# Hybrid RWKV-7 / pooling decoder block: the out-projection is split along its contraction and set beside the last quad of heads, and the quads' working tiles get fixed homes

## The chip, the cores and the metric

One core of a Trainium2 chip runs the whole block. The metric is device microseconds of one execution. Before the change three executions took 2462.72, 2460.82 and 2457.50 us, median 2460.82 us.

The engines of the core are named as in the profile: PE (TensorE, with PEld for its weight loads), DVE (VectorE), ACT (ScalarE), POOL (GpSimd) and SP (SyncE, which here issues all DMAs). Each runs its own list of instructions in order; semaphores hold an instruction until what it needs is there.

## The reference

`x` is 512 tokens by 2048, in float32. What is computed:

```
mod = silu(c) @ w_ada + b_ada                  # 6 x 2048: shift, scale, gate, twice
h   = rmsnorm(x) * (1 + sc1) + sh1
p   = h @ w_in                                 # r,k,v (3 x 1024), low-rank inputs (288), pooling input (1024)
y   = rwkv7(p[rwkv part])                      # 16 heads of 64: S = S*w + (S a) b' + v k';  y_t = S r_t
z   = pool(p[pool part])                       # 4 groups, causal means over 2,4,8,16 tokens, 256x256 matmul each
x   = x + gt1 * (concat(y, z) @ w_out)         # contraction over 2048 = 16 tiles of 128
h   = rmsnorm(x) * (1 + sc2) + sh2
x   = x + gt2 * (silu(gate) * val) @ w_down    # [val, gate] = causal conv of width 3 over h @ w_up
out = rmsnorm(x)
```

The recurrence is done in chunks of 64 tokens: in a chunk it is a triangular system, and the chunk states follow one another.

## The kernel before

All activations lie transposed: a tile is 128 features by 512 tokens. A large product is made from three matmuls of rounded parts (`mm3`, L114: high x high, high x low, low x high), so a weight tile of 128x512 (256 KB, loaded to `wraw`, L107) is first cast by ACT to its high part `whi` (L109) and subtracted by DVE to its low part `wlo` (L111). I call these L115, L116 and L117 matmuls of 512 columns **dense**: 48 of them make one output tile of 128x512 over a contraction of 16 tiles.

The program has these stages. First, adaLN shift and scale and the first eight tiles of the in-projection (L201 to L220). Then the stage that the change is about, in one PSUM layout (`mm`: 2 banks for dense outputs, `bt`: 2 double banks for the mixer, `ch`: 1 double bank for its chain):

- 27 more in-projection tiles (`win_tile`, L309). Tiles of r, k, v go through the token shift to DRAM (`win_pair`, L612) and come back a quad later.
- Four **quads** (`quad`, L362), each four heads. A quad has a front (low-rank matmuls L376 and L377, sigmoids, the scan L388, exponentials, norm of k with L405, up to `bt` L417), then scores (L427), transposed copies (L439), then the 16x16 inverses: a block of `sb` goes by DMA to DRAM and back in another layout (`dn`, `nl`, L451 and L453), DVE solves in 28 small steps (L484, L486), 24 DMAs put the inverses and their transposes in DRAM (`dx`, L492 to L494) and two DMAs read them as `X` and `Y` (L497). Two doubling levels on PE follow (L504, L513, L519), then the chain over eight chunks (L538 to L564), the outputs (L571 to L582), the group norm (L588) and the gate (L602 to L605).
- The rest of the adaLN vector, `ada_rest` (L332): 192 loads `war` of 256 KB, each multiplied by `c` and summed by one DVE instruction (L341).
- Four pooling groups (`pool_front`, `pool_back`), each fed from two in-projection tiles that come last.
- The out-projection: 16 mixer tiles `M` (L661), 16 output tiles. Eight outputs are kept in eight PSUM banks and take the contraction in blocks of four tiles (`out_block`, L666), two more follow whole, the last six in half-width matmuls (`out_half`, L759).

After it come the second norm and the MLP, which the change leaves alone.

The order of the instructions on each engine is fixed when the program is built: a list scheduler takes ready instructions, quads and pools at high priority (`hp`, L621), dense work where nothing of those is ready. What can be ready also hangs on tile buffers, which go round in program order. All quad-sized working tiles (4 KB a partition) come from one pool of 12 buffers, `q4` (L232).

Of the kernel before, what the change touches and what calls it, by code (L numbers as in the profile page):

```python
# [46 lines left out]

WIN_ORDER = ["T0", "T1", "T2", "r0", "k0", "v0", "r1", "k1", "v1"]
# [5 lines left out]
MIX_ORDER = [14, 15, 10, 11, 12, 13, 0, 1, 2, 3, 4, 5, 6, 7, 8, 9]  # L54
# [3 lines left out]
def block_kernel(ctx, tc, a, out, stop=None, dbg=None):  # L58
# [46 lines left out]
    def split_weights(src, eng=V):  # L105
        raw = wp.tile([P, WC], F32, tag="wraw", name="wraw", bufs=4)
        nc.sync.dma_start(raw, src)  # L107
        hi = wp.tile([P, WC], F32R, tag="whi", name="whi", bufs=3)
        S.copy(hi, raw)  # L109
        lo = wp.tile([P, WC], F32R, tag="wlo", name="wlo", bufs=3)  # L110
        eng.tensor_tensor(lo, raw, hi[:, :].bitcast(F32), op=ALU.subtract)  # L111
        return hi, lo
# [6 lines left out]
    def project(ps, src, acts, start=True, stop=True, engs=(V,)):  # L119

        n = len(acts)
        for k0 in range(0, n, WC // P):
            wh, wl = split_weights(src[:, k0 * P : k0 * P + WC], engs[k0 // 4 % len(engs)])
            for kk in range(WC // P):
# [47 lines left out]
    if True:  # L172
# [53 lines left out]
        if True:  # L226
# [5 lines left out]
            def quad_tile(name):  # L232
                return ra.tile([P, 2 * (16 + T)], F32, tag="q4", name=name, bufs=12)
# [7 lines left out]
            xg = two(quad_tile("xg"))  # L241
# [13 lines left out]
            rkv0 = [quad_tile(n) for n in "rkv"]  # L255
# [4 lines left out]
    def load_pw(gi):  # L260
        t = ra.tile([P, T], F32, tag="war", name="pw", bufs=3)
        pw = t.rearrange("p (i d) -> p i d", i=2)
# [3 lines left out]
    def padded(name):  # L266
        return quad_tile(name).rearrange("p (x t) -> p x t", x=2)

    def pool_front(gi, upad):
        win = WINS[gi]  # L270
        cur, lo, step = upad, 1, 1
        while step < win:
            nxt = padded("sw")
# [4 lines left out]
        z = two(quad_tile("z"))  # L278
        V.scalar_tensor_tensor(z, cur[:, :, 16:], 1.0 / win, upad[:, :, 16:], op0=ALU.mult, op1=ALU.subtract)
        V.tensor_mul(z[:, :, 0:win], cur[:, :, 16 : 16 + win], prec[:, None, 0:win].to_broadcast([P, 2, win]))  # L280
        V.tensor_sub(z[:, :, 0:win], z[:, :, 0:win], upad[:, :, 16 : 16 + win])
        return z

    def pool_back(gi, z, pw):
        ps = batch()
        mx = two(quad_tile("mxp"))
        for d in range(2):
            for i in range(2):
                PE.matmul(ps[:, d, :], pw[:, i, d * P : (d + 1) * P], z[:, i, :], start=i == 0, stop=i == 1)  # L289
            j = gi * 2 + d  # L290
            S.activation(mx[:, d, :], ps[:, d, :], AF.Identity, bias=drv[:, 35 + j : 36 + j], scale=col("psc", j))
            if gi:
                nc.sync.dma_start(mixd[8 + j], mx[:, d, :])
            else:
                last_mix.append(split_act(14 + d, mx[:, d, :]))
# [19 lines left out]
    HEADS = [(x, h) for h in range(2) for x in range(2)]  # L315

# [8 lines left out]
    dx = tc.dram_tile([2, 2, C, 2 * NK, C], F32, name="dx")  # L325
    for w in range(2):
        nc.sync.dma_start(dx[w].rearrange("s i j t -> (s i) (j t)"), sall[:, :, :, :].rearrange("p x c t -> p (x c t)"))

    cq = [None]
    modq = ra.tile([P, 4, 48], F32, tag="modq", name="modq")  # L330

    def ada_rest(n0, n1):  # L332
        for n in range(n0, n1):
            kq, j = divmod(n, 48)
            if j == 0:
                cq[0] = ra.tile([P, T], F32, tag="cq", name="cq")
                nc.sync.dma_start(cq[0], cact[0:1, kq * T : (kq + 1) * T].partition_broadcast(P))
            wa = ra.tile([P, T], F32, tag="war", name="war", bufs=3)
            nc.sync.dma_start(wa, a["ada2"][kq, j, :, :])
            jk = ra.tile([P, T], BF16, tag="jkr", name="jkr")  # L340
            V.scalar_tensor_tensor(jk, wa, 1.0, cq[0], op0=ALU.mult, op1=ALU.mult,  # L341
# [20 lines left out]
    def quad(g, rkv):  # L362
# [15 lines left out]
        sg = quad_tile("sg")  # L378
        V.memset(lead(sg)[:, :, 0:1], 0.0)
# [3 lines left out]
        al = quad_tile("al")  # L383
        for x in range(2):
            S.activation(two(al)[:, x, :], psal[:, x, :], AF.Sigmoid, bias=c2("a0", x))
        cs = quad_tile("cs")
        n = 2 * NK * (C + 1)
        V.tensor_tensor_scan(cs[:, 0:n], scanm[:, :, :].rearrange("p c t -> p (c t)"), sg[:, 0:n], 0.0,  # L388
                             op0=ALU.mult, op1=ALU.add)
        mid = ra.tile([P, 2 * NK, 1], F32, tag="mid", name="mid")  # L390
        V.tensor_copy(mid, lead(cs)[:, :, C // 2 : C // 2 + 1])
        V.tensor_sub(lead(cs), lead(cs), mid[:, :, :].to_broadcast([P, 2 * NK, C + 1]))
        ep = quad_tile("ep")
        S.activation(ep[:, 0:n], cs[:, 0:n], AF.Exp, scale=-Q)
# [591 lines left out]
```

## Time and profile before

| | us |
|---|---|
| median of three executions | 2460.82 |
| the profiled execution | 2459.58 |
| its span, first to last instruction | 2457.8 |
| PE busy in the span | 2254.7 (92%) |
| DVE busy | 1345.9 (55%) |
| ACT busy | 831.7 (34%) |
| POOL busy | 23.5 (1%) |
| share of the DMA engines (queue q1) | 44.7% |

A row of the timeline gives start, length, engine, line, operation, output <- input, shape and count; what stands in brackets is how long the engine was idle before it and what ended that. In a group or timeline row a matmul's length holds its way through the array, so dense matmuls of 0.39 us start 0.23 us apart. A matmul of 32-bit operands is two instructions in the trace, so `x64` there is 32 in the program. In a table of stretches each engine's busy time is followed by its instruction count; then come the granted PE clock, the share of the 16 DMA engines and the bytes moved.

### The profile page before, as it was taken

What the parts mean: (1) busy time and instruction counts of PE and PEld (TensorE: products, weight loads), DVE (VectorE), ACT (ScalarE), POOL (GpSimd) and SP (SyncE); (2) the same over time, 40 slices, a digit from 0 to 9 for tenths busy, and PEclk for the clock granted to TensorE, in tenths of its full rate; (3) what the DMA queues carried; (4) which work ended last, traced back from release to release, by engine and by line L of the source; (5) the groups of instructions that cost most, each with busy time, mean ns of one, the idle gap of its engine ahead of it and who ended that gap; (6) DMA issues with size and microseconds to landing.
All of it is one profiled execution on the core that took longest, in us unless ns stands there. A gap on an engine that the chain in (4) does not pass through costs nothing.

```text
span 2457.8 us, 36667 instructions
## 1 busy us (share of the span) xinstructions
PE 2254.7 (92%) x14178; PEld 1829.3 (74%) x14178; DVE 1345.9 (55%) x2398; ACT 831.7 (34%) x1351; POOL 23.5 (1%) x26
## 2 busy tenths in 40 slices
PE   4878888888379999999999999999999999999997
PEld 3656566565257889987888888888888888888887
DVE  7987686766434457757634443444344434444457
ACT  3243252523233335532223322333233322323333
POOL 0000000000000001100000000000000000000000
PEclk9989899999679999999999999999999999999998
DMA  9965757656103635538532233333323332332335
GB/s 357 340 221 163 240 176 222 213 177 208 40 32 120 198 111 181 190 105 260 170 98 98 95 98 96 99 96 97 97 97 99 95 99 95 98 97 97 99 97 174
DMA packets 204418, 352.98 MB, mean 144 GB/s; under 512 B 46033, under 2 KB 52049, under 8 KB 200017
## 3 DMA queue, kind: packets, MB, share of 16 engines
q1 hardware_dynamic: 204242, 350.63, 44.7%
q8 instruction: 111, 1.82, 0.3%
q14 instruction: 65, 0.53, 0.1%
HBM read 335.33 MB, written 15.21 MB: 143 GB/s over the span
## 4 chain that ended last, share of the span: by engine, by line
PE 63%; DMA 2%; DVE 2%; ACT 0%; issue 0%; POOL 0%; DVEq 0%; SPq 0%; ACTq 0%; POOLq 0%
PE b L115 20%; PE b L117 19%; PE b L116 19%; DMA slot<-ada 1%; DMA wraw<-wup 1%; PE bt L115 1%; PE bt L117 1%; PE bt L116 1%; DVE slot L810 1%; PE mm L115 0%; PE mm L117 0%; PE mm L116 0%; DVE wlo L111 0%; PE bt L289 0%; DVE x L863 0%
## 5 line engine op out<-in xcount | busy, mean ns | idle before, releaser
L111 DVE TENSOR_TENSOR wlo<-wraw,whi 128x512 fp32r<-128x512 f32 x772 | 532.3, 692 | 714.9 <-ACT whi L109 700.4
L109 ACT CAST whi<-wraw 128x512 fp32r<-128x512 f32 x788 | 488.5, 622 | 1240.7 <-PE b L116 931.2
L117 PE MATMUL b<-hh,wlo 128*128 128x512 f32 (+1 forms) x1472 | 560.6, 381 | 7.1 <-DVE wlo L111 6.8
L115 PE MATMUL b<-hh,whi 128*128 128x512 f32 (+1 forms) x1472 | 559.9, 380 | 0.0
L116 PE MATMUL b<-hl,whi 128*128 128x512 f32 (+1 forms) x1472 | 559.5, 380 | 0.0
L115 PE MATMUL b<-ah,whi 128*128 128x512 f32 (+1 forms) x992 | 353.3, 357 | 1.9 <-ACT whi L109 1.9
L117 PE MATMUL b<-ah,wlo 128*128 128x512 f32 (+1 forms) x992 | 352.1, 355 | 0.8 <-DVE wlo L111 0.8
L116 PE MATMUL b<-al,whi 128*128 128x512 f32 (+1 forms) x992 | 352.2, 355 | 0.0
L117 PEld LDWEIGHTS b<-hh,wlo 128*128 128x128 f32 x1472 | 277.0, 188 | 62.8 <-DVE wlo L111 9.5
L116 PEld LDWEIGHTS b<-hl,whi 128*128 128x128 f32 x1472 | 277.0, 188 | 52.5
L115 PEld LDWEIGHTS b<-hh,whi 128*128 128x128 f32 x1472 | 277.0, 188 | 52.4 <-ACT whi L109 0.6
L115 PEld LDWEIGHTS b<-ah,whi 128*128 128x128 f32 x992 | 187.7, 189 | 30.9 <-ACT ah L136 2.3
L117 PEld LDWEIGHTS b<-ah,wlo 128*128 128x128 f32 x992 | 187.7, 189 | 27.3 <-DVE wlo L111 1.2
L116 PEld LDWEIGHTS b<-al,whi 128*128 128x128 f32 x992 | 187.7, 189 | 27.2 <-DVE al L137 1.2
L117 PE MATMUL mm<-ah,wlo 128*128 128x512 f32 x464 | 190.4, 410 | 14.7 <-DVE wlo L111 14.7
L115 PE MATMUL mm<-ah,whi 128*128 128x512 f32 x464 | 189.3, 408 | 8.7 <-ACT whi L109 8.7
L116 PE MATMUL mm<-al,whi 128*128 128x512 f32 x464 | 187.7, 404 | 0.0
L341 DVE SCALAR_TENSOR_TENSOR jkr<-war,cq 128x512 bf16<-128x512 f32 x192 | 132.1, 688 | 60.9 <-DMA war<-ada 50.5
L117 PEld LDWEIGHTS mm<-ah,wlo 128*128 128x128 f32 x464 | 88.4, 191 | 43.8 <-DVE wlo L111 22.3
L848 DVE SCALAR_TENSOR_TENSOR x<-b,mod,x 128x512 f32<-128x512 f32 x80 | 59.7, 750 | 110.9 <-PE b L117 110.8
L115 PEld LDWEIGHTS mm<-ah,whi 128*128 128x128 f32 x464 | 88.7, 191 | 32.5 <-ACT whi L109 9.1
L116 PEld LDWEIGHTS mm<-al,whi 128*128 128x128 f32 x464 | 88.5, 191 | 21.7 <-issue 3.5
(267 smaller groups left out, 1926.4 us busy)
## 6 DMA issues: line engine op xcount, KB each, us to landing
wraw<-wup SPq DMA_DIRECT2D x368, 256.0 KB
war<-ada SPq DMA_DIRECT2D x192, 256.0 KB
wraw<-wdn SPq DMA_DIRECT2D x192, 256.0 KB
wraw<-win SPq DMA_DIRECT2D x140, 256.0 KB
wa<-ada SPq DMA_DIRECT2D x32, 1024.0 KB
wraw<-wout SPq DMA_DIRECT2D x88, 256.0 KB
slot<-ada SPq DMA_DIRECT2D x64, 256.0 KB
sp<-spill SPq DMA_DIRECT2D x18, 256.0 KB
```

Of the source, the lines that this page charges most:

```text
L109: S.copy(hi, raw)
L111: eng.tensor_tensor(lo, raw, hi[:, :].bitcast(F32), op=ALU.subtract)
L115: PE.matmul(ps, wh, xh, start=start, stop=False)
L116: PE.matmul(ps, wh, xl, start=False, stop=False)
L117: return PE.matmul(ps, wl, xh, start=False, stop=stop)
L341: V.scalar_tensor_tensor(jk, wa, 1.0, cq[0], op0=ALU.mult, op1=ALU.mult, accum_out=modq[:, kq, j : j + 1])
L810: V.scalar_tensor_tensor(jk, wa, 1.0, cbs[kq], op0=ALU.mult, op1=ALU.mult, accum_out=modg[:, kq, j : j + 1])
L848: V.scalar_tensor_tensor(x2[f], ps, mod[:, 80 + f : 81 + f], x2[f], op0=ALU.mult, op1=ALU.add)
```

## The change

- **In-projection order.** The eight pooling tiles are made before r, k, v of the last two head pairs; the pools are issued behind the third quad and ahead of the last quad's front, from DRAM copies `su` of their input.
- **Fixed homes.** Each quad tile has a tag of its own (`R`, `K`, `V`, `EM`, `EP`, `AL`, `INV`, `X`, `Y`, `PM`, `TB`, `TK`, `TV`) in place of the 12 shared buffers, and several steps work in place. `quad` becomes `front` and `rest`. The last quad's front is put behind the last pool's last instruction on PE, ACT and DVE (`edge`).
- **Inverse.** One DMA writes the inverses to DRAM and eight read them straight into `X`; `Y` is made from `X` by 32 matmuls with the identity and an ACT copy.
- **Matmul order.** Some loops over heads go in another order (`TURNS`); in the chain the product that does not need `ua` goes first.
- **ACT tables.** One table that has both Exp and Ln is loaded ahead (`preload_act_table_set`).
- **adaLN rest.** 96 loads of 512 KB on two buffers, in place of 192 of 256 KB on three; the multiply works in place.
- **Out-projection.** For ten output tiles, 14 of the 16 contraction tiles are done ahead (beside the last quad in program order), scaled, added to `x` and written to DRAM (`part`); later the last two tiles (the last quad's own) are added, with `part` read back as `x2`. The last six output tiles stay whole, in halves.

The core of the diff:

```diff
 WIN_ORDER = ["T0", "T1", "T2", "r0", "k0", "v0", "r1", "k1", "v1"]
-for _p in range(2, NP):
+for _p in range(2, 6):
     WIN_ORDER += [f"r{_p}", f"k{_p}", f"v{_p}"]
-WIN_ORDER += [f"u{_j}" for _j in (6, 7, 2, 3, 4, 5, 0, 1)]
+WIN_ORDER += [f"u{2 * _g + _i}" for _g in POOLS for _i in range(2)]
+for _p in range(6, NP):
+    WIN_ORDER += [f"r{_p}", f"k{_p}", f"v{_p}"]
+NM = 14
...
-            def quad_tile(name):
-                return ra.tile([P, 2 * (16 + T)], F32, tag="q4", name=name, bufs=12)
+            def cell(tag, name):
+                return ra.tile([P, WID.get(tag, 2 * T)], F32, tag=tag, name=name)
...
+        with tc.issue_after(act.ins):
+            act = S.preload_act_table_set("natural_log_exp_and_others")
...
-            wa = ra.tile([P, T], F32, tag="war", name="war", bufs=3)
+            wa = ra.tile([P, 2 * T], F32, tag="war", name="war", bufs=2)
...
-                nc.sync.dma_start(dx[0, s, e, :, e].rearrange("a j t -> j a t"), xyl[o : o + 16, 0, :, :])
-                nc.sync.dma_start(dx[1, 1 - s, e, 0:NK, e].rearrange("a j t -> j a t"), xyl[o : o + 8, 1, :, :])
-                nc.sync.dma_start(dx[1, s, e, NK:, e].rearrange("a j t -> j a t"), xyl[o + 8 : o + 16, 1, :, :])
-        X, Y = quad_tile("X"), quad_tile("Y")
-        for w, t in enumerate((X, Y)):
-            nc.sync.dma_start(flat(t), dx[w].rearrange("s i j t -> (s i) (j t)"))
+        nc.sync.dma_start(dxy, xyl[:, 0, :, :])
...
+                nc.sync.dma_start(rows(X)[o : o + 16, :, 16 * i : 16 * i + 16],
+                                  dxy[o : o + 16].rearrange("j a t -> a j t"))
+        ps = batch()
+        for c in range(NK):
+            for x, h in HEADS:
+                PE.matmul(cells(ps)[ty(h), x, c, :], slab(X)[tk(x, h), x, c, :], ident[tk(x, h), tk(x, h)],
+                          start=True, stop=True)
+        Y = cell("Y", "Y")
+        S.copy(flat(Y), wide(ps))
...
+        with hp(), ExitStack() as after:
+            for i in edge:
+                after.enter_context(tc.issue_after(i.ins))
...
+            fr = front(g, rkv)
+        with hp():
+            rest(g, rkv, fr)
+            if g == 2:
+                for gi in POOLS:
+                    edge = pool(gi)
+        ada_rest(24 * g, 24 * g + 24)
...
+    for i in range(NM):
+        load_mix(i)
+    part = []
+    for f in range(NW):
+        if f % 2 == 0:
+            xt = two(cell("K" if f % 4 == 0 else "R", "xt"))
+            nc.sync.dma_start(xt, a["xT"][:, f : f + 2, :])
+        ps = mmtile()
+        project(ps, a["wout"][f, :, 0 : NM * P], M)
+        V.scalar_tensor_tensor(xt[:, f % 2, :], ps, mod[:, 32 + f : 33 + f], xt[:, f % 2, :], op0=ALU.mult, op1=ALU.add)
+        d = tc.dram_tile([P, T], F32, name=f"part{f}")
+        nc.sync.dma_start(d, xt[:, f % 2, :])
+        part.append(d)
+    M += last_mix
...
+    for f in range(KT):
+        t = rb.tile([P, T], F32, tag=f"x2_{f}", name=f"x2_{f}")
+        nc.sync.dma_start(t, part[f] if f < NW else a["xT"][:, f, :])
+        x2.append(t)
+    for f in range(NW):
         ps = bank()
-        project(ps, a["wout"][f, :, :], M)
-        residual(f, ps, mod[:, 32 + f : 33 + f], acc, 0, T, False)
+        project(ps, a["wout"][f, :, NM * P :], M[NM:])
+        residual(f, ps, mod[:, 32 + f : 33 + f], acc, 0, T, f == 0)
```

Two places show what this does to the order of the instructions. On PE, around the last quad's front and scores, before (L405 is the norm of k, L427 and L439 scores and transposed copies, L504 the first matmul that needs the inverse; no dense matmul stands between L405 and the quad's group norm, L588):

```order
L405 MATMUL bt<-inv,cmat 128x512 x2
L427 MATMUL bt<-ar,bt__5692 64x128 x32
L439 MATMUL bt<-cmat,bt__5692 64x64 x32
L439 MATMUL bt<-cmat,kt__5748 64x64 x32
L439 MATMUL bt<-cmat,v 64x64 x32
L427 MATMUL bt<-ar,kt__5748 64x128 x32
L472 MATMUL bt<-k_5744,cmat 128x512 x2
L504 MATMUL bt<-X,sb 64x64 x32
L513 MATMUL bt<-pm,Y 64x64 x32
```

The same place in the change (L298 is the pools' matmul, L380 the low-rank one, L411 the norm, L442, L454, L490, L501 and L509 the score block, L118 to L120 dense matmuls, here of the out-projection):

```order
L298 MATMUL mm<-z,pw 128x512 x8
L379 MATMUL bt<-xwa,lw 64x512
L380 MATMUL bt<-xwa,lw 64x512
L379 MATMUL bt<-xwa,lw 64x512
L380 MATMUL bt<-xwa,lw 64x512
L379 MATMUL bt<-xwa,lw 64x512
L380 MATMUL bt<-xwa,lw 64x512
L379 MATMUL bt<-xwa,lw 64x512
L380 MATMUL bt<-xwa,lw 64x512
L411 MATMUL bt<-inv,cmat 128x512 x2
L442 MATMUL bt<-ar,inv 64x128 x32
L454 MATMUL bt<-cmat,inv 64x64 x32
```

And from the last part of the score block on (L501 scores, L509 the bonus sum):

```order
L454 MATMUL bt<-cmat,v 64x64 x32
L501 MATMUL bt<-ar,sg 64x128 x32
L509 MATMUL bt<-al,cmat 128x512 x2
L118 MATMUL mm<-ah_6968,whi 128x512
L119 MATMUL mm<-al_6969,whi 128x512
L120 MATMUL mm<-ah_6968,wlo 128x512
```

From the last two pools' matmuls to the end of the score block no dense matmul is left; behind L509 dense work now stands in the quad, where before there was none. On SP, around the last quad's inverse, before (`dx` and `X`, `Y` as above; no `war` load is left by then):

```order
L492 DMA dx<-xyl 16x16x16
L493 DMA dx<-xyl 8x16x16
L494 DMA dx<-xyl 8x16x16
L497 DMA X<-dx 128x1024
L497 DMA Y<-dx 128x1024
L107 DMA wraw<-win 128x512
```

and in the change (`war` are the adaLN loads of 512 KB, `part` the written partial sums):

```order
L343 DMA war<-ada 128x1024 x2
L110 DMA wraw<-wout 128x512
L527 DMA dxy_6329<-xyl 128x256
L110 DMA wraw<-wout 128x256
L343 DMA war<-ada 128x1024
L531 DMA X<-dxy_6329 16x16x16 x8
L343 DMA war<-ada 128x1024 x2
L730 DMA part_7120<-xt 128x512
L730 DMA part_7190<-xt 128x512
L343 DMA war<-ada 128x1024 x2
```

The 24 `dx` writes are gone, and `war` loads now stand in front of, between and behind the inverse's DMAs of the last quad.

More of the change, by code (lines that the diff above doesn't have):

```diff
@@ L260, in load_pw, with padded, pool @@
     def load_pw(gi):
-        t = ra.tile([P, T], F32, tag="war", name="pw", bufs=3)
-        pw = t.rearrange("p (i d) -> p i d", i=2)
+        t = ra.tile([P, 2 * T], F32, tag="war", name="pw", bufs=2)
+        pw = t[:, 0:T].rearrange("p (i d) -> p i d", i=2)
         nc.sync.dma_start(pw, a["poolw"][gi, :, :, :])
         return pw
-    def padded(name):
-        return quad_tile(name).rearrange("p (x t) -> p x t", x=2)
-    def pool_front(gi, upad):
+    def padded(t):
+        return t.rearrange("p (x t) -> p x t", x=2)
+    def pool(gi):
         win = WINS[gi]
+        pw = load_pw(gi)
+        upad = padded(cell("K", "upad"))
+        V.memset(upad[:, :, 0:16], 0.0)
+        for i in range(2):
+            nc.sync.dma_start(upad[:, i, 16:], su[gi, i])
         cur, lo, step = upad, 1, 1
         while step < win:
-            nxt = padded("sw")
+            nxt = padded(cell("EP" if step in (1, 4) else "EM", "sw"))
             V.tensor_add(nxt[:, :, lo:], cur[:, :, lo:], cur[:, :, lo - step : 16 + T - step])
@@ L315, in block_kernel @@
     HEADS = [(x, h) for h in range(2) for x in range(2)]
+    TURNS = [(x, h) for x in range(2) for h in range(2)]
     def tk(x, h):
@@ L324, in block_kernel @@
     G.memset(sall, 0.0)
[L325 to L327 removed]
     cq = [None]
[L330 removed]
+    modq = ra.tile([P, 2, 48], F32, tag="modq", name="modq")
     def ada_rest(n0, n1):
@@ L360, in cells, with front @@
         return ps[:, :, :].rearrange("p x (c t) -> p x c t", t=C)
-    def quad(g, rkv):
+    def front(g, rkv):
         r, k, v = rkv
@@ L406, in quad @@
         V.tensor_scalar_max(flat(inv), wide(psn), 1e-24)
-        S.activation(flat(inv), flat(inv), AF.Ln)
-        S.activation(flat(inv), flat(inv), AF.Exp, scale=-0.5)
+        with tc.issue_after(act.ins):
+            S.activation(flat(inv), flat(inv), AF.Ln)
+            S.activation(flat(inv), flat(inv), AF.Exp, scale=-0.5)
         for x in range(2):
@@ L411, in quad, with rest, c2 @@
                                    op0=ALU.mult, op1=ALU.mult)
+        return lws, al, ep, em, inv, fdec
+    def rest(g, rkv, fr):
+        r, k, v = rkv
+        lws, al, ep, em, inv, fdec = fr
+        def c2(name, x):
+            return col(name, 2 * g + x)
         ar = ra.tile([P, 2 * NK, 2, C], F32, tag="ar", name="ar")
@@ L624, in block_kernel @@
     shift(win_tile(8), 17, two(rkv0[2])[:, 1, :])
-    rkv = rkv0
+    edge = []
     for g in range(NQ):
-        if g + 1 < NQ:
-            win_pair(2 * g + 2)
-            win_pair(2 * g + 3)
-        with hp():
+        if g < NQ - 1:
+            if g == 2:
+                for n, gi in enumerate(POOLS):
+                    for i in range(2):
+                        ps = win_tile(21 + 2 * n + i)
+                        t = ra.tile([P, T], F32, tag="spill", name="spill", bufs=2)
+                        S.copy(t, ps)
+                        d = tc.dram_tile([P, T], F32, name=f"su{gi}_{i}")
+                        nc.sync.dma_start(d, t)
+                        su[gi, i] = d
+            at = (9, 15, 29)[g]
+            win_pair(2 * g + 2, at)
+            win_pair(2 * g + 3, at + 3)
+        with hp(), ExitStack() as after:
+            for i in edge:
+                after.enter_context(tc.issue_after(i.ins))
+            rkv = rkv0
```

232 lines of the change are left out of this document (107 added, 125 removed).

## The prediction

> **What bounds the kernel now.** I read the page first: its span, PE's row of forty slices and the granted clock's.
>
> ```profile
> span 2457.8 us, 36667 instructions
> ...
> PE   4878888888379999999999999999999999999997
> ...
> PEclk9989899999679999999999999999999999999998
> ```
>
> A slice is 61.4 us. From slice 13 (about 740 us) PE is full to the end, and the MLP there is not touched. What can change lies ahead, above all in slices 11 and 12, where PE has 3 and 7 tenths. Next the table of stretches, cut at the quads:
>
> ```profile
> core 0: us, PE busy (x) PEld busy (x) DVE busy (x) ACT busy (x) POOL busy (x), PEclk, DMA share, GB/s
> 163.00:302.00 139.00, 119.41 (x1467) 88.35 (x1467) 100.53 (x241) 43.37 (x73) 0.00 (x0) 0.93 0.64 198
> ...
> 451.00:601.00 150.00, 129.20 (x1504) 92.33 (x1503) 103.10 (x247) 52.70 (x85) 0.00 (x0) 0.97 0.66 207
> 601.00:635.00 34.00, 17.22 (x62) 8.39 (x64) 18.38 (x23) 22.31 (x27) 0.00 (x0) 0.76 0.19 63
> 635.00:672.00 37.00, 12.57 (x352) 10.44 (x348) 15.33 (x39) 2.96 (x3) 0.00 (x0) 0.64 0.19 43
> 672.00:726.00 54.00, 38.37 (x822) 30.21 (x814) 19.38 (x36) 16.77 (x33) 0.00 (x0) 0.70 0.01 3
> 726.00:814.00 88.00, 87.89 (x354) 65.95 (x355) 38.84 (x59) 29.67 (x48) 0.00 (x0) 1.00 0.39 126
> ```
>
> The last quad (601 to 726 us) stands alone: the DMA is idle, DVE too for over half the time, and the granted clock is low. Behind it PE is full. In the first quads PE is busy 86% of the time and DVE 70%. Then PE's timeline, for the borders:
>
> ```profile
> 163.05 1.11 PE L376 MATMUL bt<-xwa,lw 64*64 64x512 f32 x1 [8.35 <-DVE k L229]
> ...
> 394.42 1.16 PE L504 MATMUL bt<-X,sb 64*64 64x64 f32 x64 [1.32 <-DMA X<-dx]
> ...
> 402.87 2.51 PE L519 MATMUL bt<-Y,pm 64*64 64x64 f32 x64
> ...
> 600.61 1.93 PE L588 MATMUL bt<-rs,cmat 128*128 128x512 f32 x4
> ...
> 613.63 1.93 PE L377 MATMUL bt<-xwa,lw 64*64 64x512 f32 x8 [0.77 <-DVE rs L606]
> ...
> 620.88 3.78 PE L405 MATMUL bt<-inv,cmat 128*128 128x512 f32 x4 [4.88 <-ACT inv L404]
> ...
> 634.62 3.69 PE L427 MATMUL bt<-ar,bt__5692 64*64 64x128 f32 x64 [9.97 <-DVE bt__5692 L417]
> ...
> 671.25 1.99 PE L504 MATMUL bt<-X,sb 64*64 64x64 f32 x64 [22.62 <-DMA X<-dx]
> ...
> 714.30 3.68 PE L588 MATMUL bt<-rs,cmat 128*128 128x512 f32 x4 [2.48 <-ACT rs L585]
> ...
> 725.90 0.50 PE L605 MATMUL bt<-xgh,gw 128*128 128x512 f32 x1 [0.71 <-DVE gw L601]
> ...
> 812.86 1.98 PE L289 MATMUL bt<-z,pw 128*128 128x512 f32 x4
> ...
> 904.69 0.39 PE L117 MATMUL b<-ah,wlo 128*128 128x512 f32 x1
> ...
> 911.49 0.39 PE L117 MATMUL b<-ah,wlo 128*128 128x512 f32 x1
> 911.71 0.28 PE L115 MATMUL b<-ah,whi 128*128 128x256 f32 x1
> ```
>
> Between the L117 rows at 904.69 and 911.49 lie 30 starts of dense matmuls, so one takes 6.80/30 = 0.2267 us. The half-width outputs begin at 911.71; from there on both kernels do the same.
>
> **The frame of the sum.** From 163.05 to 911.71 are 748.66 us. Both kernels must do the same 1776 full-width dense matmuls there (27 in-projection tiles x 48, ten outputs x 48): 402.6 us. The other 346.1 us are the mixer's own matmuls and PE's waits, and only they can change. By the order of before's instructions 986 dense stand ahead of the third quad's L588 (600.61), 40 from there to 725.90, and 750 behind. So the 346.1 divide into 437.56 - 223.5 = 214.1 (three quads), 125.29 - 9.1 = 116.2 (the last quad), and 185.81 - 170.0 = 15.8 (the rest). In the changed order 811 dense stand ahead of the third quad's squares, 485 from there to the last in-projection tile, 170 in the last quad between scores and squares, 250 behind, and then 60 of the second pass. I cost its stages in this order.
>
> **First three quads: 214.1 becomes 201.** Four things change. The switches of ACT's table first, by their groups:
>
> ```profile
> L408 ACT ACT_TABLE_LOAD x4 | 5.1, 1283 | 0.1
> L590 ACT ACT_TABLE_LOAD x4 | 5.1, 1283 | 0.1
> ```
>
> And ACT's timeline at the third quad's group norm:
>
> ```profile
> 602.61 1.28 ACT L589 ACT_TABLE_LOAD   x1 [1.61 <-PE bt L588]
> 603.91 1.11 ACT L589 ACTIVATE rs<-bt,eps 128x1024 f32<-128x1024 f32 x1
> ```
>
> Of a quad's loads three (L408, L589, L590) go whose results the next step waits for, 3 x 1.283 us, in three quads -11.6. The one that is loaded ahead lies beside the scan.
>
> The Trainium skill's page "ScalarE: Activation LUTs", section "What ACT_TABLE_LOAD costs", adds 1.38 us of drain to each switch, by which this term would be -24. The trace doesn't agree: the load ends at 603.89 and the activation starts at 603.91, so I keep to the row.
>
> Second, the new order of heads: the 64 matmuls of L519 take 2.51 us in the old order, those of L504, which alternate as TURNS does, 1.16. Two such steps a quad give 2 x 1.35 x 3 = -8.1. Third, the adaLN steps. DVE's groups:
>
> ```profile
> L111 DVE TENSOR_TENSOR wlo<-wraw,whi 128x512 fp32r<-128x512 f32 x772 | 532.3, 692 | 714.9 <-ACT whi L109 700.4 <-DMA x<-xT 4.1 <-PE mm L117 3.5
> L341 DVE SCALAR_TENSOR_TENSOR jkr<-war,cq 128x512 bf16<-128x512 f32 x192 | 132.1, 688 | 60.9 <-DMA war<-ada 50.5 <-DMA cq<-cact 6.1 <-DMA dx<-xyl 2.2
> L207 DVE SCALAR_TENSOR_TENSOR jk<-wa,cb 128x2048 bf16<-128x2048 f32 x32 | 73.1, 2285 | 0.0
> L341 DVE DVE_READ_ACCUMULATOR jkr<-war,cq 128x1 f32 x192 | 15.7, 82 | 0.0
> ```
>
> A step of 512 columns takes 0.69 + 0.08 = 0.77 us. One of 1024 lies between 512 and L207's 2048; on the line through both it is 0.688 + (2.285 - 0.688)/3 = 1.22, with the read 1.30 us. Before, 19 to 24 steps stand between solve and `y` of each early quad; after, none in the second and third quad: 2 x 20 x 0.77 = 31 us of DVE work leave the chain. I take a quarter as on the path, -8 (bounds 0 and -31). Against them, fewer dense matmuls cover the inverse's way: 121, 99 and 73 ahead of X in place of about 150, 6.6 to 17.5 us less cover, 35 together. The way gets shorter as well, since 24 small DMAs go; I take 14.6 of the 35 as new waiting (bounds 0 and 35). 214.1 - 11.6 - 8.1 - 8 + 14.6 = 201.
>
> **Third quad's gate and the first two pools: 15.** This has dense work beside it (443 dense matmuls in one piece in the new order), so I take the amount that before's rest needed, 15.8 with its 16 pool matmuls, less a little.
>
> **Last two pools and the last quad's front: 38.** Nothing dense is left here. The front waits for the pools by its edge. A pool's own steps:
>
> ```profile
> L274 DVE TENSOR_TENSOR sw<-upad 128x1054 f32<-128x1054 f32 x4 | 5.0, 1252 | 2.0 <-ACT upad L645 2.0
> L279 DVE SCALAR_TENSOR_TENSOR z<-sw,upad 128x1024 f32<-128x1024 f32 x4 | 4.9, 1223 | 0.1
> ```
>
> Two to four sums of 1.25, one of 1.22 and the matmuls of 1.98 (row at 812.86) make 6 to 8 us for a pool, the second half hidden by the first: 11. The front took 634.62 - 613.63 = 21.0. To it come 10 splits and a wide adaLN step on DVE (8.2, of which I take 5), half a weight landing (2.1), less a table load (-1.3): 37.8.
>
> **Last quad, scores to squares: 111, less the dense work in it.** Before: 714.30 - 634.62 = 79.7, bare. DVE's rows about the inverse:
>
> ```profile
> 650.49 0.42 DVE L478 TENSOR_TENSOR xyl<-nl,lanei 128x256 f32<-128x256 f32 x1 [2.78 <-DMA nl<-dn]
> ...
> 658.54 0.38 DVE L487 COPY xyl<-xyl 128x256 f32<-128x256 f32 x1
> ```
>
> The solve takes 8.4 us alone. Put among it are 7 adaLN steps and 6 splits: 7 x 1.30 + 6 x 0.69 = +13. Eight more adaLN steps stand in the score block; a third of their 10.4 us, +3. The DMAs after the solve took 671.25 - 658.92 = 12.3 us; nine in place of 26 I put at 7, -5 (from -8 to +10, since one SP queue now has 512 KB loads ahead of them). 32 matmuls for Y +2, TURNS -3. Then the chain: 19 adaLN steps (24.7 us) and nine splits (6.2) come into 43 us (671.25 to 714.30) in which DVE was busy about a third. Whatever waits for an instruction of the chain now waits behind one of 1.30 us; I take two thirds of the 31 as delay, +21. Together 111; the 170 dense matmuls in it are 38.5, so 72 remain. The low bound of +21 is 6, if gaps take nearly all; the high one comes from the loads. There are two buffers, so a step is not had more often than every (landing + 1.30)/2. Landings of 256 KB under load, from the chain of waits:
>
> ```profile
> 972.03 4.62 DMA wraw<-wout
> 983.13 4.27 DMA wraw<-wup
> ```
>
> With 4.6 us for 512 KB the 19 steps take 56 us, less than the 64 that I have; with 9.2, twice as much, 100.
>
> **Gate and second pass: 14.** Before, 11.6 us (714.30 to 725.90) with 9.1 of dense; I take 6, as PE starts and stops. In the second pass the 16 tiles of x are loaded (4 MB) ahead of most of its weights. At 207 GB/s for a share of 0.66 (row 451 to 601) full rate would be 313 GB/s, 13.4 us. Four weight buffers of six matmuls cover 5.4; 8 remain (0 if the loads land in the long run of dense work before it).
>
> Sum: 201 + 15 + 38 + 72 + 14 = 340, against 346.1: -6. On the profiled execution's 2459.58 that is 2453.5; the median of the runs shown lies 1.24 above it, so I forecast **2455**. What large gain was there, 116 us of the last quad, is mostly not taken up: its front stays bare, and 50 wide adaLN loads move beside its chain.
>
> **Rivals.** *Cover works fully* (2426). The dense matmuls of the last quad hide the chain's new DVE work (+21 becomes 0), and the way of the inverse costs no new waiting in the early quads (8 of the 14.6): -29. For it: DVE has half of 672 to 726 free, and DMA stands at 0.01. Against it: DVE works in order, and a chain step has one successor.
>
> *The adaLN loads hold the last quad* (2478, slower). Place: DVE between solve and `y`, last quad. Each of the 19 steps stands ahead of a chain step, and waits for a load that has just two buffers. It decides from a 512 KB landing of 2 x 64/19 - 1.30 = 5.4 us on; at 7.9, between one and two of the loaded 256 KB landings, the 19 steps take 87 us, 23 more than I have. For it: L341's row shows 50.5 us idle for `war` with three buffers and half the size, and out-projection weights use the same queue there. Against it: early quads load at 0.66 of the DMA's time.
>
> *The early quads' gains are hidden* (2460). Tables and TURNS then lie under dense matmuls (19.7 not gained), while the inverse's shorter way keeps inside its cover (14.6 not lost): +5. For it: PE's wait at 394.42 is 1.32 us only.
>
> **How the numbers follow.** Forecast 0.45 (its own range 2442 to 2466), full cover 0.20, loads 0.22, hidden gains 0.13. The range leaves out the outer half of the second and third: 2424 to 2479. A measurement of this kernel tells about 0.2%, 4.9 us, from no change. Below 2455.9 lie 0.27 of the forecast's 0.45, the 0.20 and 0.03 of the last: faster 0.50. Within: 0.15 + 0.08 = 0.23. Slower: 0.03 + 0.22 + 0.02 = 0.27.
>
> **What would show it.** Right: in the profile after, ACT's table loads fall to about 28; the last quad's front shows PE idle for some 20 us; solve to `y` there takes about 64 us plus the solve's 21; PE waits about 8 us for weights after the ten part sums. Wrong: a `war` wait of DVE that totals over 20 us in the last quad (the loads), or a PE clock of 0.9 and more there with gaps below 30 us (full cover).

## The result and the profile after

| | before | after |
|---|---|---|
| median of four executions, us | 2459.16 | 2430.41 |
| ratio, with its 95% interval | | 0.9887 (0.9857 to 0.9916) |
| span of the profiled execution, us | 2457.8 | 2426.3 |

The change made the kernel faster by 28.75 us, 1.1%. The forecast was 2455 (range 2424 to 2479). The page after, in the rows that the prediction started from:

```profile
span 2426.3 us, 36875 instructions
...
PE   4778899899857989999999999999999999999997
...
PEclk9989999999979999999999999999999999999998
```

Two weak slices are left, the twelfth and thirteenth with 5 and 7 tenths, where before the eleventh and twelfth had 3 and 7. The early slices went up as well, from mostly 8 to 8 and 9. PE's timeline after, at the borders of the same stages (L380 low-rank matmuls, L630 squares, L442 scores, L118 the half-width outputs):

```profile
162.12 1.11 PE L380 MATMUL bt<-xwa,lw 64*64 64x512 f32 x1
...
523.07 1.98 PE L630 MATMUL bt<-rs,cmat 128*128 128x512 f32 x4
...
681.97 3.69 PE L442 MATMUL bt<-ar,inv 64*64 64x128 f32 x64 [15.99 <-DVE inv L433]
...
794.81 1.98 PE L630 MATMUL bt<-rs,cmat 128*128 128x512 f32 x4
...
880.77 0.28 PE L118 MATMUL b<-ah,whi 128*128 128x256 f32 x1
```

I take from each stretch its dense matmuls at 0.2267 us, as in the prediction, and call the rest **bare** time:

| bare us | before | forecast | after |
|---|---|---|---|
| three early quads | 214.1 | 201 | 360.95 - 811 x 0.2267 = 177.1 |
| third quad's gate, pools, last front | (29.0) | 53 | 158.90 - 485 x 0.2267 = 49.0 |
| last quad, scores to squares | 79.7 | 72 | 112.84 - 170 x 0.2267 = 74.3 |
| its gate and the second pass | (23.3) | 14 | 85.96 - 310 x 0.2267 = 15.7 |
| sum | 346.1 | 340 | 316.0 |

(The two in brackets are cut at the same instructions of before; its own 16 pool matmuls lie in the second of them.) Three of four stages came out within 4 us of the forecast. The whole miss is in the early quads: 24 us more than forecast went away there. So I put the experiments mainly on them, and a few on what the last quad costs.

How the early quads stand, part by part, bare us (the order gives the dense matmuls of each part; front is L376/L380 to scores, way from the end of the scores to X, levels from X to the first matmul with `sk`, chain from there to the squares; the third quad's gate after the change has the in-projection beside it and is left out):

| | front | scores | way of the inverse | levels | chain | gate |
|---|---|---|---|---|---|---|
| second quad before | 7.1 | 11.2 | 7.8 | 14.1 | 23.3 | 9.2 |
| second quad after | 3.9 | 9.9 | 5.8 | 11.1 | 17.4 | 7.4 |
| third quad before | 7.0 | 10.2 | 10.3 | 13.5 | 22.9 | 8.3 |
| third quad after | 4.8 | 11.2 | 3.0 | 14.1 | 17.0 | |

PE's waits in the early quads, before (163 to 601 us) and then after (162 to 523 us), as engine, tile, line, releaser: total, times, longest:

```profile
PE mm L117 <- DVE wlo L111: 14.7, 13, 2.9
PE mm L115 <- ACT whi L109: 8.7, 3, 3.9
```
```profile
PE mm L120 <- DVE wlo L114: 4.1, 4, 2.2
```

Before, dense matmuls waited 23.4 us there for a split of weights, of which 14.7 was DVE's half; after, 4.1. The share of DVE shows in the table of stretches, for before and for after:

```profile
163.00:601.00 438.00, 375.63 (x4467) 273.34 (x4468) 308.44 (x738) 149.51 (x242) 0.00 (x0) 0.95 0.65 204
```
```profile
162.00:523.00 361.00, 325.33 (x4483) 236.08 (x4483) 238.00 (x438) 129.42 (x217) 2.87 (x3) 0.97 0.50 153
523.00:682.00 159.00, 136.10 (x554) 101.05 (x554) 69.43 (x101) 56.57 (x87) 0.00 (x0) 0.94 0.50 160
682.00:795.00 113.00, 86.29 (x1367) 65.76 (x1368) 85.11 (x168) 26.04 (x51) 0.00 (x0) 0.86 0.79 244
795.00:881.00 86.00, 78.56 (x324) 62.30 (x324) 46.48 (x82) 27.91 (x51) 0.00 (x0) 0.94 0.57 190
```

In the early quads DVE is busy 70 us less and the DMA's share falls from 0.65 to 0.50; in the last quad DVE is now busy 85 of 113 us and the DMA at 0.79. This is the adaLN rest, which moved.

### The profile page after: what moved, and what is told of

It is laid out like the page before. It is cut to its first block, busy times and chain, and to the rows that moved or that the text cites. A ratio compares the mean times of both kernels' runs of the same rounds, so it can differ in the third digit from the quotient of the medians.

```text
span 2426.3 us, 36875 instructions
## 1 busy us (share of the span) xinstructions
PE 2250.7 (93%) x14434; PEld 1825.1 (75%) x14434; DVE 1344.6 (55%) x2230; ACT 817.7 (34%) x1349; POOL 27.3 (1%) x30
## 3 DMA queue, kind: packets, MB, share of 16 engines
q1 hardware_dynamic: 186322, 354.69, 45.7%
## 4 chain that ended last, share of the span: by engine, by line
PE 74%; DVE 11%; DMA 9%; issue 3%; ACT 2%; SPq 1%; DVEq 0%; POOL 0%; ACTq 0%
PE b L118 20%; PE b L120 20%; PE b L119 20%; DMA war<-ada 4%; PE mm L120 4%; PE mm L118 4%; PE mm L119 3%; DVE jk L211 3%; DVE war L344 2%; DMA slot<-ada 1%; DVE wlo L114 1%; DMA wraw<-wup 1%; PE mm L298 1%; PE bt L561 0%; ACT ah L147 0%
## 5 line engine op out<-in xcount | busy, mean ns | idle before, releaser
L114 DVE TENSOR_TENSOR wlo<-wraw,whi 128x512 fp32r<-128x512 f32 (+1 forms) x782 | 534.9, 685 | 717.7 <-ACT whi L112 710.9
L112 ACT CAST whi<-wraw 128x512 fp32r<-128x512 f32 (+1 forms) x798 | 491.0, 616 | 1275.4 <-PE b L119 923.4
L120 PE MATMUL b<-hh,wlo 128*128 128x512 f32 (+1 forms) x1472 | 560.7, 381 | 7.2 <-DVE wlo L114 6.9
L118 PE MATMUL b<-hh,whi 128*128 128x512 f32 (+1 forms) x1472 | 559.9, 380 | 0.0
L118 PE MATMUL b<-ah,whi 128*128 128x512 f32 (+1 forms) x980 | 350.0, 357 | 4.5 <-ACT whi L112 3.5
L120 PE MATMUL b<-ah,wlo 128*128 128x512 f32 (+1 forms) x980 | 348.7, 356 | 4.7 <-DVE wlo L114 4.7
L120 PEld LDWEIGHTS b<-hh,wlo 128*128 128x128 f32 x1472 | 277.0, 188 | 62.6 <-DVE wlo L114 9.4
L118 PEld LDWEIGHTS b<-hh,whi 128*128 128x128 f32 x1472 | 277.1, 188 | 52.6 <-ACT whi L112 0.5
L118 PE MATMUL mm<-ah,whi 128*128 128x512 f32 x572 | 232.3, 406 | 10.7 <-ACT whi L112 10.7
L120 PE MATMUL mm<-ah,wlo 128*128 128x512 f32 x572 | 232.2, 406 | 4.9 <-DVE wlo L114 4.9
L119 PE MATMUL mm<-al,whi 128*128 128x512 f32 x572 | 230.2, 402 | 0.0
L118 PEld LDWEIGHTS b<-ah,whi 128*128 128x128 f32 x980 | 186.0, 190 | 34.1 <-ACT whi L112 6.0
L120 PEld LDWEIGHTS b<-ah,wlo 128*128 128x128 f32 x980 | 186.0, 190 | 31.4 <-DVE wlo L114 5.8
L119 PEld LDWEIGHTS b<-al,whi 128*128 128x128 f32 x980 | 186.1, 190 | 26.9 <-DVE al L141 1.2
L344 DVE SCALAR_TENSOR_TENSOR war<-war,cq 128x1024 f32<-128x1024 f32 x96 | 117.0, 1222 | 54.6 <-DMA war<-ada 53.9
L118 PEld LDWEIGHTS mm<-ah,whi 128*128 128x128 f32 x572 | 109.1, 191 | 38.7 <-ACT whi L112 11.5
L120 PEld LDWEIGHTS mm<-ah,wlo 128*128 128x128 f32 x572 | 109.0, 191 | 33.9 <-DVE wlo L114 8.9
L119 PEld LDWEIGHTS mm<-al,whi 128*128 128x128 f32 x572 | 109.1, 191 | 24.3 <-issue 1.7
```

Of the source, the lines that this page charges most:

```text
L112: S.copy(hi[:, 0:w], raw[:, 0:w])
L114: eng.tensor_tensor(lo[:, 0:w], raw[:, 0:w], hi[:, 0:w].bitcast(F32), op=ALU.subtract)
L118: PE.matmul(ps, wh, xh, start=start, stop=False)
L119: PE.matmul(ps, wh, xl, start=False, stop=False)
L120: return PE.matmul(ps, wl, xh, start=False, stop=stop)
L344: V.scalar_tensor_tensor(wa, wa, 1.0, cq[0], op0=ALU.mult, op1=ALU.mult, accum_out=modq[:, kq, j : j + 1])
```

## The experiments

Two theories on the early quads. **A**: the mixer's own path got shorter, by the tables, the order of heads and the inverse. **B**: the adaLN steps left. Each run's ratio is to the kernel before on the same chip; the changed kernel's is 0.9887 (0.9857 to 0.9916).

One thing about what these numbers can tell. The early quads hold the same instructions, with the same dense matmuls beside each quad, in the change, ada_loads_only, pools_bt, split_behind and ada_before_last. Their bare time there was 177.1, 175.9, 181.3, 182.7 and 182.9 us, one profiled execution each. So a difference under 7 us in the sum of the three early quads tells nothing by itself, and the change's 177.1 is near the low end.

### What each part is worth when it is undone

**tables_undone**

```diff
-        with tc.issue_after(act.ins):
-            act = S.preload_act_table_set("natural_log_exp_and_others")
```

> The changed kernel without the table that is loaded ahead: 28 table loads in the block in place of 14. Theory A (the mixer's own path in the quads got shorter by the tables, the order of heads and the inverse, and PE waits for that path): 14 loads of 1.283 us come back on it, 18 us, so about 2448 us, and the three early quads hold 10 to 14 us more of non-dense PE time. Theory B (the early quads gained because DVE was freed of the adaLN steps, and the loads lie beside dense work): only the loads in the last quad's bare front and gate count, 3 to 5 us, so about 2434 us, early quads within 4 us.

Measured: 0.9983 (0.9967 to 0.9998), about 24 us slower than the change. Borders of the early quads, here the first low-rank matmul and the third quad's squares:

```profile
164.01 1.11 PE L379 MATMUL bt<-xwa,lw 64*64 64x512 f32 x1 [7.80 <-DVE k L233]
...
542.54 1.88 PE L628 MATMUL bt<-rs,cmat 128*128 128x512 f32 x4
```

That is 378.5 us with 819 dense matmuls, 192.9 bare: +15.8 against the change, +10 to +17 against the runs with the same early quads. Last quad +6.5. A holds. The largest groups of table loads after, ten of the fourteen that are left of 30:

```profile
L390 ACT ACT_TABLE_LOAD x4 | 5.1, 1283 | 0.1
L159 ACT ACT_TABLE_LOAD x3 | 3.8, 1283 | 3.0 <-PE pst L154 2.9
L383 ACT ACT_TABLE_LOAD x3 | 3.8, 1283 | 0.0
```

**turns_undone**

```diff
-    TURNS = [(x, h) for x in range(2) for h in range(2)]
+    TURNS = HEADS
```

> The changed kernel with the old order of heads in every loop (TURNS = HEADS). Theory A: two steps a quad take 2.5 us in place of 1.1, and the state products of the chain as well: 3 us in each quad, 12 in all, so about 2442 us. Theory B: the matmuls get longer in the trace but the chain is set by its hops between PE, ACT and DVE: under 4 us, about 2432 us.

Measured: 0.9912 (0.9896 to 0.9929), an interval that overlaps the change's. Its second quad has 57.1 us bare against 55.5, its third without the gate 49.8 against 50.1. The first quad is no measure: split_behind, which has the same instructions there, differs from the change by 5.3 us in it (76.8 to 71.5), and turns_undone gives 76.7. So under 2 us in the two quads that can be compared, no more than pools_bt shows there without this edit (57.3 in the second); theory B's "under 4" holds. The groups of the reordered product over the whole run, in the change and in before, show why:

```profile
L561 PE MATMUL bt<-Y,pm 64*64 64x64 f32 x512 | 21.0, 250 | 3.8 <-DVE pm L549 3.6 <-issue 0.2
```
```profile
L519 PE MATMUL bt<-Y,pm 64*64 64x64 f32 x512 | 20.4, 245 | 5.5 <-DVE pm L507 5.5
```

Its eight pieces (two a quad) take 21.0 us in the new order and 20.4 in the old: the order does not shorten it.

**inverse_undone**: the 24 writes and two reads of before in place of one and eight, and Y by DMA.

```diff
...
-        nc.sync.dma_start(dxy, xyl[:, 0, :, :])
...
+                nc.sync.dma_start(dx[0, s, e, :, e].rearrange("a j t -> j a t"), xyl[o : o + 16, 0, :, :])
...
+            nc.sync.dma_start(flat(t), dx[w].rearrange("s i j t -> (s i) (j t)"))
```

> The changed kernel with the inverse as before: 24 writes and two reads through DRAM, Y by DMA. The scheduler then puts 148 and 153 dense matmuls ahead of X in the first two quads (121 and 99 in the change). Theory A: the way is 5 to 6 us longer in every quad, and dense matmuls that cover it are missing later; about 5 us a quad, 20 in all, so about 2450 us. Theory B: the way is covered in the early quads all the same, and only the last quad pays: 6 us, about 2436 us.

Measured: 0.9949 (0.9932 to 0.9965), about 15 us slower. The early quads have 179.7 bare, 2.6 more and inside their spread: the second quad's way is longer, but 152 dense matmuls stand beside it in place of 98. The last quad loses 4.1, and the stretch behind it 5.5; PE waits 10.3 us for weight splits there, in place of 6.6. That this comes from dense matmuls spent earlier as cover is not shown. The total lies between the two expectations.

**split_behind**: the partial out-projection held until the last quad's last matmul.

```diff
...
-        project(ps, a["wout"][f, :, 0 : NM * P], M)
+        with tc.issue_after(tail.ins):
+            project(ps, a["wout"][f, :, 0 : NM * P], M)
```

> The changed kernel with the partial out-projection's matmuls held until the last quad's last matmul. Forecast: the 170 dense matmuls in the last quad (38.5 us) then run behind it, and the last quad keeps 112 us less the relief of DVE (nine splits, 6 us): 30 to 35 us slower, about 2463 us. Rival (the dense matmuls in the chain delay it by about as much as they fill, since the chain waits for PE behind them): the last quad gets shorter by 20 us or more, so about 2445 us.

Measured: 1.0051 (1.0031 to 1.0070), about 40 us slower than the change, and slower than before. PE's scores, X and squares of the last quad there:

```profile
687.51 3.69 PE L442 MATMUL bt<-ar,inv 64*64 64x128 f32 x64 [14.45 <-DVE inv L433]
...
735.53 0.44 PE L536 MATMUL bt<-cmat,X 64*64 64x64 f32 x2 [32.14 <-DMA X<-dxy]
...
795.34 3.78 PE L630 MATMUL bt<-rs,cmat 128*128 128x512 f32 x4 [3.94 <-ACT rs L627]
```

Without any dense matmul the quad takes 107.8 us from scores to squares; with 170 of them 112.8. So 38.5 us of work cost 5 us there. The rival (that they delay the chain by what they fill) falls. And the bare 107.8 is 28 us more than the 79.7 in before, with the adaLN steps in it and net of the quad's other changes. ada_in_quads and ada_before_last below take the steps out alone.

### Where the adaLN steps stand

**before_less_ada**

```diff
+    G.memset(modq, 0.0)
...
-        ada_rest(48 * g, 48 * g + 48)
+        if g < 1:
+            ada_rest(48 * g, 48 * g + 48)
```

> The kernel before, with three quarters of the adaLN loads and their steps left out (the first 48 of 192 stay, with the first quad), so the MLP gets a wrong shift, scale and gate. Theory B: its second and third quad get 15 to 20 us shorter by that alone, about 2441 us. Theory A: under 8 us, about 2453 us. The last quad has no such step before and stays as it is in both.

Measured: 0.9772 (0.9757 to 0.9786), 56 us faster than before, far more than either expected. The borders of its early quads (line numbers are one higher than in before):

```profile
163.08 1.11 PE L378 MATMUL bt<-xwa,lw 64*64 64x512 f32 x1
...
539.65 1.91 PE L589 MATMUL bt<-rs,cmat 128*128 128x512 f32 x4
```

The early quads come to 177.3 us bare, from 214.0: the second and third (this one without its gate) give 14.5 and 15.6 of it. The other 20 us come behind. The third quad's gate and the last quad's front have 14.2 less, as more dense matmuls were left for the front (77 in place of 1), and the last quad itself 5.2 less, with 31 dense matmuls in it. The expectation that it would stay as it is does not hold. B holds, and the two quads give about twice what it expected of them at the low end.

**ada_in_quads**: the pools' weights get tiles of their own, so the adaLN loads no longer queue behind them for two buffers.

```diff
-        t = ra.tile([P, 2 * T], F32, tag="war", name="pw", bufs=2)
+        t = cell(dict(zip(POOLS, ("PM", "TV", "Y", "X")))[gi], "pw")
```

> The changed kernel with the pools' weights in tiles of the quad that are free then, and no longer in the adaLN loads' two buffers, so that the adaLN loads are not held up behind the pools: by its order 21 and 7 wide steps stand between solve and y in the second and third quad again (none in the change), and none in the last quad. Theory B (the early quads gained because DVE was freed): they get 12 to 20 us longer, the last quad 28 us shorter (107.8 us bare with the loads against 79.7 without, as measured), so about 2418 us. Theory A (the early quads gained by the mixer's own path): early quads within 5 us, so about 2407 us. Rival for the last quad (the dense matmuls set its length now): it falls by less than 10 us.

Measured: 0.9838 (0.9818 to 0.9858), 2419.03 us, as B said; its interval touches the change's by its edge. The third quad's end, and the last quad's scores and squares:

```profile
576.88 1.92 PE L630 MATMUL bt<-rs,cmat 128*128 128x512 f32 x4
...
704.65 3.69 PE L442 MATMUL bt<-ar,inv 64*64 64x128 f32 x64 [12.72 <-ACT al L475]
784.74 1.88 PE L630 MATMUL bt<-rs,cmat 128*128 128x512 f32 x4
```

Early quads 202.7 (+25.6; 20.8 of it in the second and third, the rest within the first quad's own spread; more than B's 12 to 20), last quad 80.1 us long and 43.6 bare (-30.7).

**ada_before_last**: the second half held until the third quad's last DVE instruction.

```diff
...
+            if g >= 2:
+                after.enter_context(tc.issue_after(hold.ins))
```

> As ada_in_quads, but the second half of the adaLN loads is held until the third quad's last DVE instruction: early quads as in the change, 43 steps beside the last in-projection tiles, none in the last quad. If the adaLN steps lengthen the last quad's chain, it falls by 25 to 30 us and the stretch of the in-projection tiles stays within 5 us, so about 2404 us. If the loads are too much for the DMA there (26 MB more in 120 us), PE waits for weights, 10 to 20 us are given back, about 2418 us.

Measured: 0.9875 (0.9860 to 0.9889), no different from the change. Last quad 45.7 (-28.6), but gate, pools and front 71.1 (+22.1). PE's waits from 523 to 682 us:

```profile
PE mm L298 <- ACT ah L140: 5.9, 1, 5.9
PE mm L120 <- DVE wlo L114: 4.3, 5, 2.6
PE mm L298 <- DVE spill L233: 3.2, 1, 3.2
```

PE waits for spills and splits. Over 523 to 659 us DVE is busy 86.6 us there, 51.2 in the change, and the DMA's share is 0.81 in place of 0.46. Which of the two makes PE wait is not told apart, so the second expectation (the loads are too much there) may have its part. The second half of this work costs about 20 to 31 us of PE's time in each of the three places tried.

**ada_loads_only**

```diff
+            if kq:
+                V.tensor_copy(modq[:, kq, j : j + 1], wa[:, 0:1])
+                continue
```

> The changed kernel with the second 48 adaLN loads kept and waited for, but the DVE step of 1024 columns replaced by a copy of one column (the sums of those loads are left out). By its order 4 and 17 of them stand in the last quad's solve and chain. If DVE's own work of the steps sets the last quad's length, it falls from 74 us of non-dense time to about 48, as it did with the loads elsewhere: about 2405 us. If the waits for the loads set it (two buffers), it stays at 65 or more: 2420 us or more.

Measured: 0.9903 (0.9880 to 0.9926), no different from the change. The last quad's scores and squares (line numbers are three higher here):

```profile
680.70 3.53 PE L445 MATMUL bt<-ar,inv 64*64 64x128 f32 x64 [14.95 <-DVE inv L436]
...
775.09 1.12 PE L633 MATMUL bt<-rs,cmat 128*128 128x512 f32 x2
```

It has 77.8 us bare, as the second expectation said. DVE's waits in the whole span:

```profile
DVE modq L345 <- DMA war<-ada: 58.8, 34, 4.8
DVE war L347 <- DMA war<-ada: 25.6, 23, 3.3
```

DVE now stands still 58.8 us for those loads and 25.6 for the first 48, 84.4 together, where the change waits 53.9 for all 96. Of the 46.9 us of work that left DVE (1344.6 to 1297.7 busy), 30.5 came back as waiting. But the scheduler put only 73 dense matmuls into this quad, not 170, and its length fell from 112.8 to 94.4, against 82.2 in ada_before_last with no such step. Read by its length, the steps' work makes 18 of 31 us and the loads the rest; read by bare time, all of it is the loads.

Its parts tell more. DVE's solve takes 22.1 us in the change, 9.3 here and 8.0 in ada_before_last, so in the solve it is the steps' work. From X to the squares there are 65.7, 57.1 and 48.3 us; in the chain alone 44.2, 36.5 and 31.0, with 86, 62 and 61 dense matmuls beside it. So the loads alone lengthen the chain by 5.5 us at equal dense work. How much of the rest is whose stays open.

### The tables alone, and a better version

**before_tables**

```diff
+        with tc.issue_after(act.ins):
+            act = S.preload_act_table_set("natural_log_exp_and_others")
...
+        with tc.issue_after(act.ins):
+            S.activation(ep[:, 0:n], cs[:, 0:n], AF.Exp, scale=-Q)
...
```

> The kernel before with nothing changed but the table that is loaded ahead (14 table loads in place of 30). If the loads lie on the path that PE waits for in the early quads also there, as undoing them in the changed kernel showed (15.8 us in the early quads, 23 to 24 in all), it gains about that: 2436 us. If the adaLN steps on DVE set the pace of these quads in before, the path gets shorter for nothing: under 8 us, 2452 us or more.

Measured: 0.9914 (0.9894 to 0.9933), 2438.48 us, 19 to 21 us faster than before. That is about two thirds of the change's gain, from two lines (and Exp and Ln held behind them). Only 7.8 of it show as bare time in the early quads (206.2); 11.7 lie in the last quad's gate and front, where now 44 dense matmuls stand in the front. The early quads themselves got 17.2 us shorter (437.6 to 420.4), with 945 dense matmuls beside them in place of 986. So part of what the path saved there moved dense work to where PE was idle. Whether the adaLN steps hid some of the table loads in before is not shown by this.

**pools_bt**

```diff
+        ps2 = batch()
...
-            ps = mmtile()
+            ps = ps2[:, d, :]
```

> The changed kernel with the pools' matmuls in the mixer's PSUM tiles (bt) in place of the dense ones (mm). By its order the pools no longer wait behind the last in-projection tiles, and 230 dense matmuls stand in the last quad's front. If the mm tiles kept pools and front bare, their 49 us of non-dense time fall to about 27, so about 2408 us. If the front is held by the k tiles, which come from the last in-projection tiles through DRAM, less than 10 us are gained, about 2423 us.

Measured: 0.9861 (0.9843 to 0.9878), which overlaps the change. Dense matmuls now stand in the front, but PE still waits there:

```profile
PE bt L443 <- DVE inv L434: 11.8, 1, 11.8
PE bt L412 <- ACT inv L411: 5.9, 2, 4.4
```

Pools and front 51.7, no gain; some 30 adaLN steps went into that front, and quads_x2late_bt below, without them, gains there. The last quad gains 10.6 (63.7).

**quads_x2late**: ada_in_quads, and each tile of x loaded just ahead of its weights.

```diff
...
+        nc.sync.dma_start(x2[f], part[f])
         project(ps, a["wout"][f, :, NM * P :], M[NM:])
```

> ada_in_quads with each tile of x for the second pass loaded just ahead of its own weights, and not all 16 ahead of them. If the wait of PE there (3.9 and 1.9 us in the changed kernel) comes from those 16 loads in one piece, the stretch behind the last quad gets 4 to 6 us shorter than 14.0: about 2414 us. If each output waits for its own load instead, nothing is gained: 2419 us.

Measured: 0.9830 (0.9807 to 0.9852); the total can't be told from ada_in_quads, but the stretch behind the last quad has 8.7 us bare, from 14.0.

**quads_x2late_bt**: both.

> quads_x2late with the pools' matmuls in the mixer's PSUM tiles as well. Without adaLN steps in the last quad's front the dense matmuls set there should cover it: pools and front fall from 46 us of non-dense time to 30 or less, about 2400 us. If the front's wait is for the k tiles through DRAM, they stay above 40: 2412 us.

Measured: 0.9801 (0.9778 to 0.9824), 2409.54 us: faster than the change, whose interval it doesn't touch, and 48 us faster than before. Its third quad's squares and its last quad's scores:

```profile
577.09 1.91 PE L631 MATMUL bt<-rs,cmat 128*128 128x512 f32 x4
...
696.00 3.69 PE L443 MATMUL bt<-ar,inv 64*64 64x128 f32 x64
```

Pools and front take 118.9 us with 364 dense matmuls, 36.4 bare (47.9 without bt), between the two expectations.

## Why the prediction was right or wrong

The time, 2430, is in the range and faster, which had the largest chance. That it is in the range is luck in part. The forecast's own 2455, with 2442 to 2466, is 25 us off, and the range reaches down to 2424 only for the rival of full cover at 2426. Of that rival's two halves one came: the way of the inverse cost no new waiting in the early quads. The other did not: the last quad kept 74.3 us where that rival had about 50. What made up the difference are other terms, below.

**Early quads, 201 against 177.1: wrong.** Three of the four terms failed.

- *adaLN, "a quarter as on the path, -8"*: much too small, though inside its bounds. ada_in_quads puts it at 20.8 and before_less_ada at 30.1 for the same two quads. I costed only the steps between solve and `y`. They also stood in the solve (13 and 14 before, 3 and 0 after, by the order), which took 21.3 and 22.7 us before and 13.6 and 9.8 after. And they stood ahead of the weight splits: dense matmuls waited 14.7 us for DVE's half before and 4.1 after.
- *cover, "14.6 of the 35 as new waiting"*: wrong in sign. The bare time on the way fell in the three quads, from 6.6, 7.8 and 10.3 us to 3.9, 5.8 and 3.0. The way itself went from 40.6, 41.4 and 44.5 us to 31.3, 28.3 and 19.6. In the second and third quad the shorter solves give 7.7 and 12.9 us of that; how much is due to fewer DMAs, and how much to less dense work beside it, was not taken apart. I counted the cover that went and not the solve that got shorter.
- *TURNS, -8.1*: close to nothing. I took the time of another matmul group (1.16) for what the reordered one would reach, but it still takes 2.0 us or more in every place, and its eight pieces take 21.0 us after against 20.4 before. Undone, the order of heads costs under 2 us in two quads, where I had 5.4.

*Tables, -11.6*, was right as far as the runs tell: 10 to 17 us by tables_undone, 7.8 bare by before_tables. Between the first low-rank matmul and the third quad's squares 15 loads stand before and 5 after, so ten went, where I had counted nine. The sign that I gave, loads falling to about 28, did not fit that count: 12 fewer in four quads would leave 18, and there are 14.

tables_undone has nine more loads than the change in that stretch; at 1.283 us they are 11.5. With the drain of 1.38 us that the Trainium skill adds to each switch ("ScalarE: Activation LUTs", "What ACT_TABLE_LOAD costs") they would be an estimated 24. No run here shows that drain: in before, 18 of the 30 loads start 0.02 us after the activation ahead of them ends, and the next one starts 0.01 us after the load.

**Pools and front, 53 against 49.0: right, by its terms too.** The gate and the first two pools have 13.0 (forecast 15), and from the last two pools' first matmul (at 646.00) to the scores there are 36.0 (38). The bare wait stands where it was forecast: 15.99 us ahead of L442, row at 681.97.

**Last quad, 72 against 74.3: right in its sizes, but not all of the cause is shown.** DVE's solve there:

```profile
700.57 0.28 DVE L515 COPY xyl<-nl 128x256 f32<-128x256 f32 x1
...
722.27 0.38 DVE L525 COPY xyl<-xyl 128x256 f32<-128x256 f32 x1
```

It takes 22.1 us, 13.7 more than alone (forecast +13); from its end to X (729.14) 6.5 us (forecast 7); from X to the squares 65.7 (forecast 64). Without adaLN steps the quad has 28.6 to 30.7 us less bare time (ada_before_last, ada_in_quads), where the forecast had 13 + 3 + 21 = 37, splits included. The dense matmuls cost 5. I had the +21 as DVE's work; ada_loads_only shows that waiting for the loads is part of it.

**Gate and second pass, 14 against 15.7: right in size and place, cause partly open.** I had 8 us of waiting, for 4 MB at the DMA's rate; PE waits 5.75. SP's queue shows that the issues themselves take time:

```profile
860.30 4.97 SPq L793 DMA_DIRECT2D x<-part  x10
865.31 3.83 SPq L793 DMA_DIRECT2D x<-xT  x6
```

Sixteen issues in 8.8 us, and PE's waits of 3.89 (row at 871.67 below) and 1.86 right behind them:

```profile
871.67 0.80 PE L120 MATMUL b<-ah,wlo 128*128 128x512 f32 x1 [3.89 <-DVE wlo L114]
875.61 0.80 PE L118 MATMUL b<-ah,whi 128*128 128x512 f32 x1 [1.86 <-ACT whi L112]
```

quads_x2late took 5.3 us away with the same bytes, so the loads in one piece ahead of the weights are what PE waits for, as forecast. Whether it was their issue time or their bytes, that run doesn't tell.

**Rivals.** The slower one (loads hold the last quad) named a real wait, and it is not ruled out as a part. Its time, 2478, did not come, and a load of 512 KB landed after 4.5 us in the median in the last quad (3.3 to 6.5), under the 5.4 from which it was to decide:

```profile
war<-ada SPq DMA_DIRECT2D x35, 512.0 KB, 4.5
```

But the sign that I had given for it, a `war` wait of DVE over 20 us in the last quad, stands just at its border:

```profile
DVE war L344 <- DMA war<-ada: 20.1, 17, 2.5
```

Of these 20.1 us, 15.4 lie between X and the squares. There 21 steps take 65.7 us, one in 3.1 us, where two buffers with such landings allow one in (4.5 + 1.30)/2 = 2.9. So the loads come close to setting the pace of the steps there. The rival that nothing is gained early falls: the early quads lost 37 us of bare time.

## What to carry to other kernels

Low-priority work on a shared in-order engine is not free beside a chain: every step of it can hold up whoever is queued behind it, here also the splits that feed the dense matmuls meant as cover. Before pricing such steps by their place in the chain, count them in every list ahead of which something waits, and ask what the stage would take without them; leaving them out in one run shows the bound. Moving them from one busy place to another may gain little: here each of three places cost about 20 to 31 us. And the cover that is lost must be set against the new length of what it covered, not the old.

## What the runs showed that I had not expected

A chain without adaLN steps repeats almost to a tenth: the second quad's had 17.4, 17.4, 17.5 and 17.3 us bare in after, split_behind, turns_undone and ada_before_last. The first quad's chain, which has them, had 22.8 to 26.9 in the runs with the same instructions there. Much of the spread of this kernel's times may come from how the loads fall, which was not tested by itself.

The clock granted to PE in the last quad was higher where dense matmuls stood in it: 0.65 in before (635 to 714 us) and 0.61 in split_behind (688 to 795), with none; 0.86 in the change (682 to 795), with 170. The four matmuls of the squares take 3.68 us in before and 3.78 in split_behind, at the quad's end, and 1.98 in the change. So dense work set into the gaps also made the quad's own matmuls faster here.
